# A ninth weight buffer in the place of the transposed activations, and cache pages looked up four at a time

## The chip, the cores and the metric

The kernel runs on one core of a Trainium2 chip. The metric is device time in microseconds (us) of one execution, and each kernel is timed in several runs whose median counts. Five engines work side by side, each through its own queue of instructions in order: TensorE (PE, with its weight loads PEld), VectorE (DVE), ScalarE (ACT), GpSimd (POOL) and SyncE (SP). SP here only issues DMA transfers and looks up the addresses that they need. SBUF is the on-chip memory in which tiles lie, PSUM the memory into which TensorE writes.

## The reference

One step of a hybrid decoder layer on 288 tokens: 256 of a prompt and 8 requests of 4 new tokens each. Cut to what matters here:

```python
u = rmsnorm(h, g_mix)
q_lat, q_rope, lat, k_rope, x_br, y_br = mixer_projections(u, ...)
# prompt: causal attention over its 256 tokens
# samples: 16 cached pages of 128 positions per request, found by a page table
lat_past = cache_latent[page_table]; rope_past = cache_krope[page_table]
s = (q_lat @ lat.T + q_rope @ k_rope.T) * SM_SCALE
o_lat = softmax(s) @ lat
o_rec = rglru(causal_conv(x_br))               # a recurrence over the tokens
h = h + concat(rmsnorm(o_mla), rmsnorm(gelu(y_br) * o_rec)) @ w_o
# 32 experts of three 2048 x 512 matrices; each token uses 2 of them
h = h + sum_e combine[:, e] * (silu(t @ w_gate[e]) * (t @ w_up[e])) @ w_down[e]
h = h + sigmoid(rmsnorm(h) @ w_ple_gate + b) * (p @ w_ple_proj)
y = rmsnorm(h)
```

The outputs are y, the new latent rows and rotated keys, and the last states of the recurrence and of the convolution. All is float32; the expert matrices alone are 403 MB, read once.

## The kernel before

**Front part (0 to 470 us).** The dense projections run as products of 128 x 128 weight blocks with 288 token columns. A weight tile of 512 KB is loaded into `wraw` (`load`, L207; three buffers), split into a high and a low part (`whi` by ACT, L219; `wlo` by DVE, L220), and three matmuls per block (L229 to L231) add up the product: 24 matmuls for each `wraw` tile. After each tile `dense3` calls `hook`, and with it `tick`, which lets other work in: steps of the recurrence, and the sample attention.

The sample attention has 16 units (`sample`, `fetch`), one started every second tick. A unit takes four requests and two pages of each: 8 pages of 288 KB, read into four `kv` buffers out of 12 (`KVB`). For each page SP reads its number out of the page table (L488) and issues the DMA (L490). Then TensorE computes scores `Ss` (L503, L507), DVE and ACT make the softmax (`ms`, `Ssb`; L512 to L532), TensorE transposes it (`tp`, L538), DVE copies it out (`pTs`, L539) and TensorE multiplies it with the page (`Os`, L550). These names are the ones in the rows below; `pg`, `xc`, `gr`, `gi`, `yb` and `xx` belong to the recurrence.

In this part a scheduler orders the instructions of every engine while the program is built, from the order of the calls and its own idea of what is ready; the queues then run in that order.

At its end the residual `hT` (128 x 16 x 288, 18 KB per partition) holds h, token columns side by side. `post` (L902, L908) reads each of its 16 blocks once more: for the router's logits, and to transpose it into `hn`, in which tokens are rows. After that nothing reads or writes `hT` until the down projections add to it.

**Expert part (470 to 1100 us).** Experts are taken in ten units, 0 to 9: units 0, 3, 5 and 7 hold two experts (wide), the others four. `front` runs over four quarters of the 2048 inputs, first for `w_gate`, then for `w_up`; `wload` takes the next slot of a ring (`slots`, `wslot`) and issues a DMA of 2 MB for two experts (L1012). The ring has eight slots: five in a pool that opens when the front part's operands are released (`ws1`, w0 to w4), two more in a pool behind them (`ws3`), and one where the router's small tiles lay (`ws4`). A slot is loaded again when TensorE has read it. `gather` picks each expert's tokens out of `hn` with one-hot matmuls (`xp`, L1054). Small jobs are put in between by two lists: `front` takes one entry of `steps` per block under `w_gate`, one of `more` under `w_up`. Behind unit `OVU` (3) stands `overflow`, a branch that is taken only if an expert has more tokens than its place holds; it reads a flag on every engine (L1225).

**Down part (1100 to 1452 us).** `down` reads `w_down` through the ring's five `ws1` slots and adds to `hT` (L1131); here TensorE's order is as written. The last 47 us are the gated embedding and the final norm.

Of the kernel before, what the change touches and what calls it, by code (L numbers as in the profile page):

```python
# [21 lines left out]
NP = 256  # L22
# [12 lines left out]
KVB = 12  # L35
AHEAD = 2
NSQ = 2
NNQ = 0
# [8 lines left out]
HEAVY = 4  # L47
OVU = 3
XXW = 3 + NP + 7 * NR
# [67 lines left out]
def hymba_kernel(ctx, tc, a):  # L117
# [53 lines left out]
    tmp = pool(st_tmp, "tmp")  # L171
    wps = [pool(st_w, "wp"), 3, 3, 2]
    up = pool(st_u, "up")
# [4 lines left out]

    lane, queue, clock = [], [], [0]

    def tick():

        for g in list(lane):
            if next(g, 1):
                lane.remove(g)
        if queue:
            clock[0] += 1
            if clock[0] <= AHEAD or (clock[0] - AHEAD) % PACE == 0 or clock[0] >= DENSE:
                start()
# [125 lines left out]
    dma(C, a["cst"])  # L315
    ptk = za.tile([1, 128], I32, name="ptk")
    dma(ptk, a["table"])
    uh = up.tile([128, KD, NTOK], F32R, name="uh")
# [140 lines left out]

    sa = pool(st_sa, "sa")  # L460
    pq = psF([128, 2, H, 32], "pq")

# [16 lines left out]
    last = [None] * 2  # L479

    def fetch(u):
        g, v = divmod(u, 8)
        L = []
        for j in range(4):
            kv = sa.tile([128, 2, 576], F32, name="kv", bufs=KVB)
            for x in range(2):
                c = 16 * (4 * g + j) + 2 * v + x
                page = nc.values_load(ptk[0:1, c:c + 1], engines=[mybir.EngineType.SP], min_val=0,  # L488
                                      max_val=a["cache"].shape[0] - 1)
                dma(kv[:, x, :], a["cache"][bass.ds(page, 1)].rearrange("o p c -> (o p) c"))  # L490
            L.append(kv)
        return L

    def sample(u):

        L = fetch(u)
        g, v = divmod(u, 8)
# [65 lines left out]
    def finish(g, m):  # L563
# [20 lines left out]
    def prompt_pool():  # L584
# [9 lines left out]
        for b in range(2):  # L594
            wuvp.append([pa.tile([128, 2, 4, 128], F32R, name="wv" + nm) for nm in "hl"])
            halves(*wuvp[b], wuv[:, :, 4 * b:4 * b + 4, :])
            for t in range(2):
                p = psK([128, 512], "vv")
                for c in range(2):
                    x = [y[:, c, t * 128:(t + 1) * 128] for y in lp_]  # L600
                    mm3(p, *x, *(y[:, c].rearrange("p h v -> p (h v)") for y in wuvp[b]), c == 0, c == 1)
                nc.scalar.copy(vv[:, t, 4 * b:4 * b + 4, :].rearrange("p h v -> p (h v)"), p)
            r = pa.tile([128, 2, 4, 128], F32, name="wr")
            dma(r, a["wuk"][:, :, 4 * b:4 * b + 4, :])
            wk.append([pa.tile([128, 2, 4, 128], F32R, name="wk" + nm, bufs=2) for nm in "hl"])
            halves(*wk[b], r)
            yield
# [101 lines left out]
    class Part:  # L709
# [19 lines left out]
        def begin(self):  # L729
            n = self.n  # L730
            self.xs = self.xx[:, :, 3 + NP:].rearrange("p c (r s) -> p c r s", s=7)
            self.cvs = lp.tile([128, 2, NR, 3], F32, name="cvs")
            self.xc = lp.tile([128, 2, CW], F32, name="xc")
# [6 lines left out]
                "p c (r s) -> p c r s", s=3))  # L740
            nc.vector.tensor_copy(self.cvs, self.xs[:, :, :, 4:])

        def conv(self, c):
# [19 lines left out]
        def decay(self):  # L763
            n = self.n
            dma(cp_d[:, 2 * n:2 * n + 2], self.xx[:, :, NP:3 + NP])
            dma(cs_d[:, 2 * n:2 * n + 2], self.cvs)
            gr, t2, th = self.gr, self.t2, self.th
            nc.scalar.activation(th, gr, AF.Tanh)
            nc.scalar.activation(t2, gr, AF.Exp, scale=2.0)
            nc.scalar.activation(gr, gr, AF.Exp)  # L770
            nc.vector.scalar_tensor_tensor(t2, t2, 1.0, th, op0=ALU.add, op1=ALU.mult)
# [13 lines left out]
        def state(self):  # L785
# [4 lines left out]
            if n == 3:  # L790
                dma(a["lru_p"], lrp[:, :8])
                dma(a["lru_s"], lrp[:, 8:])

        def gelu(self):
# [130 lines left out]
    ws3 = pool(st_w3, "ws3")  # L925
    slots = [(ws1, f"w{i}") for i in range(WB1)] + [(ws3, f"w{WB1 + i}") for i in range(WB3)]

# [72 lines left out]
    def wslot(i=0):  # L1000
        p_, nm = slots.pop(i)
        return p_.tile([128, 2, 4, 512], F32, name=nm), (p_, nm)

# [215 lines left out]

    more += [lambda: None] * 4 + [lambda: reorder(rkT, rks), limits, weights]  # L1220

# [386 lines left out]
def layout(inp):  # L1608
# [16 lines left out]
    for n in range(4):  # L1625
# [13 lines left out]
        cr.reshape(-1, 2, 64, 64).transpose(0, 1, 3, 2).reshape(-1, 128, 64), cl], 2)  # L1639
    A["table"] = f["page_table"].reshape(1, -1)  # L1640
    w = f["w_o"][0]
# [48 lines left out]
```

## Time and profile before

| | us |
|---|---|
| median of 3 runs (1497.66 to 1500.59) | 1499.51 |
| the profiled execution's own time | 1500.35 |
| its span, first to last instruction | 1498.7 |
| TensorE busy | 1300.5 (87%) |
| VectorE, ScalarE busy | 553.5, 392.0 |
| mean traffic | 346 GB/s over the span |

The span is 1.65 us shorter than the time, and the profiled execution is 0.84 us above the median. Engines work at once, so busy times don't add up to the span. "Idle before" is time in which an engine did nothing right before an instruction, with what it waited for last. A DMA's share of 1.00 means that all 16 DMA engines were busy throughout.

### The profile page before, as it was taken

To read this page: it belongs to the slowest core of one execution; us is meant where nothing else is said; L and a number is where in the kernel's file an instruction comes from. 1 tells how busy PE (TensorE), PEld (TensorE's weight loads), DVE (VectorE), ACT (ScalarE), POOL (GpSimd) and SP (SyncE) were. 2 spreads that over 40 slices of the span, in tenths; PEclk is the share of its full clock that TensorE was granted. 3 is DMA by queue.
4 is the path that set the end of the run, shared out by engine and by line. 5 is a ranking of instruction groups with operands and counts; after the bars stand their busy time and mean duration, and the time that the engine had idled before them with its cause. 6 is when DMAs were issued, how large, how long until landed. Compare 5 with 4: busy or idle time off the path is not lost.

```text
span 1498.7 us, 24037 instructions
## 1 busy us (share of the span) xinstructions
PE 1300.5 (87%) x9535; PEld 851.1 (57%) x9535; DVE 553.5 (37%) x1322; ACT 392.0 (26%) x744; POOL 23.1 (2%) x26
## 2 busy tenths in 40 slices
PE   7999888799999988775978868869778999999996
PEld 7997677588996444222523423416235666666675
DVE  6765545666663100000000000003023455555557
ACT  6535434655441100000000000002013322222335
POOL 0000000000000000000000000000000000000014
PEclk9999998999999999987999989979899999999997
DMA  7879787532776899999999999999999999999971
GB/s 271 275 242 295 240 277 246 160 141 76 266 273 266 352 396 427 428 427 428 417 428 427 428 428 427 427 426 426 393 418 419 419 419 419 419 419 418 420 287 64
DMA packets 80841, 518.32 MB, mean 346 GB/s; under 512 B 10705, under 2 KB 12818, under 8 KB 47826
## 3 DMA queue, kind: packets, MB, share of 16 engines
q1 hardware_dynamic: 80066, 514.33, 86.3%
q0 software_dynamic: 656, 2.39, 0.4%
q8 instruction: 77, 1.26, 0.3%
q14 instruction: 42, 0.34, 0.1%
HBM read 513.81 MB, written 2.88 MB: 345 GB/s over the span
## 4 chain that ended last, share of the span: by engine, by line
DMA 35%; PE 15%; DVE 2%; issue 1%; ACT 0%; DVEq 0%; SPq 0%; ACTq 0%
DMA w<-in_w_down 21%; DMA w<-in_w_up 8%; PE Gp L1081 6%; DMA w<-in_w_gate 5%; PE xp L1054 4%; PE Y L1114 2%; PE pp L1280 1%; DMA wpp<-in_w_pp 1%; DVE gtt L1492 1%; DVE hT L1495 0%; DVE gtt L1487 0%; DVE hT L1596 0%; PE yp L1129 0%; PE s L1464 0%; PE acc L1460 0%
## 5 line engine op out<-in xcount | busy, mean ns | idle before, releaser
L1081 PE MATMUL Gp<-w,Xq 128*32 128x512 f32 (+1 forms) x2048 | 356.8, 673 | 93.4 <-DMA w<-in_w_up 50.1
L1081 PEld LDWEIGHTS Gp<-w,Xq 128*32 128x32 f32 (+1 forms) x2048 | 89.7, 127 | 318.7 <-issue 175.9
L229 PE MATMUL acc<-uh,whi 128*128 128x288 f32 x496 | 155.6, 314 | 14.9 <-ACT whi L219 7.4
L231 PE MATMUL acc<-uh,wlo 128*128 128x288 f32 x496 | 153.8, 310 | 3.5 <-DVE wlo L220 3.4
L230 PE MATMUL acc<-ul,whi 128*128 128x288 f32 x496 | 152.4, 307 | 0.4 <-DVE ul L264 0.4
L1090 DVE SCALAR_TENSOR_TENSOR Yb<-Gp,rs,Yb 128x512 f32<-128x512 f32 x10 | 7.5, 751 | 341.8 <-PE Gp L1081 307.5
L1131 DVE TENSOR_TENSOR hT<-hT,yp 128x288 f32<-128x288 f32 x160 | 71.2, 450 | 165.2 <-PE yp L1129 165.2
L1054 PE MATMUL xp<-Pq,hn 96*128 96x256 f32 (+1 forms) x576 | 119.8, 360 | 12.8 <-issue 12.0
L1114 PE MATMUL Y<-w,w 128*32 128x256 f32 (+1 forms) x1280 | 113.8, 389 | 19.2 <-DMA w<-in_w_down 19.1
L1054 PEld LDWEIGHTS xp<-Pq,hn 96*128 96x128 f32 x576 | 97.2, 197 | 53.9 <-issue 42.6
L229 PEld LDWEIGHTS acc<-uh,whi 128*128 128x128 f32 x496 | 97.9, 197 | 19.0 <-ACT whi L219 9.2
L220 DVE TENSOR_TENSOR wlo<-wraw,whi 128x1024 fp32r<-128x1024 f32 x82 | 99.9, 1220 | 18.6 <-PE acc L231 9.8
L231 PEld LDWEIGHTS acc<-uh,wlo 128*128 128x128 f32 x496 | 98.0, 198 | 7.4 <-DVE wlo L220 5.8
L219 ACT CAST whi<-wraw 128x1024 fp32r<-128x1024 f32 x82 | 85.4, 1042 | 63.9 <-PE acc L230 45.5
L230 PEld LDWEIGHTS acc<-ul,whi 128*128 128x128 f32 x496 | 98.2, 198 | 1.6 <-DVE ul L264 0.9
L1114 PEld LDWEIGHTS Y<-w,w 128*32 128x32 f32 (+1 forms) x1280 | 51.7, 116 | 66.2 <-DMA w<-in_w_down 34.1
L1058 DVE TENSOR_SCALAR Xq<-xp,P 128x256 f32<-128x256 f32 (+1 forms) x48 | 21.1, 440 | 168.5 <-PE xp L1054 168.5
L1118 ACT ACTIVATE Yh<-Y,wsl 128x256 fp32r<-128x256 f32 x80 | 37.9, 473 | 173.6 <-PE Y L1114 172.9
L1089 ACT ACTIVATE Yb<-Gp,rs 128x512 f32<-128x512 f32 x10 | 6.9, 687 | 283.9 <-PE Gp L1081 278.4
L1114 PE MATMUL Y<-w,wl 128*32 128x256 f32 (+1 forms) x768 | 72.3, 389 | 8.9 <-DMA w<-in_w_down 8.9
L1056 ACT ACTIVATE Xq<-xp,P 128x256 f32<-128x256 f32 (+1 forms) x48 | 21.0, 438 | 189.8 <-PE xp L1054 189.8
L231 PE MATMUL acc<-gh,wlo 128*128 128x288 f32 x224 | 66.1, 295 | 1.3 <-DVE wlo L226 1.3
(487 smaller groups left out, 1868.8 us busy)
## 6 DMA issues: line engine op xcount, KB each, us to landing
w<-in_w_gate SPq DMA_DIRECT2D x64, 2048.0 KB, 26.0
w<-in_w_up SPq DMA_DIRECT2D x64, 2048.0 KB, 24.8
w<-in_w_down SPq DMA_DIRECT2D x128, 1024.0 KB, 17.1
kv<-in_cache SPq DMA_DIRECT2D x128, 288.0 KB, 3.9
wraw<-in_w_in SPq DMA_DIRECT2D x44, 512.0 KB, 4.8
wraw<-in_w_o SPq DMA_DIRECT2D x32, 512.0 KB, 4.0
wraw<-in_w_pg SPq DMA_DIRECT2D x30, 512.0 KB, 15.2
wraw<-in_w_uq SPq DMA_DIRECT2D x6, 512.0 KB, 4.1
```

What stands on the lines that cost most here:

```text
L219: nc.scalar.copy(hi[:, x, :], r[:, x, :])
L220: nc.vector.tensor_sub(lo[:, x, :], r[:, x, :], hi[:, x, :].bitcast(F32))
L229: nc.tensor.matmul(out, hi, xh, start=start, stop=False)
L230: nc.tensor.matmul(out, hi, xl, start=False, stop=False)
L231: nc.tensor.matmul(out, lo, xh, start=False, stop=stop)
L1054: nc.tensor.matmul(xp, hn[:, t, d * 128:(d + 1) * 128], Pq[:, t, :n], start=t == 0, stop=t == 2)
L1056: nc.scalar.activation(X[:, d, :n], xp, AF.Copy, scale=prm("g_ffn", d))
L1058: nc.vector.tensor_scalar(X[:, d, :n], xp, prm("g_ffn", d), None, op0=ALU.mult)
L1081: nc.tensor.matmul(acts[j][sl * e:sl * e + sl, :], X[:, kk, o:o + sl], wt[e](k), start=kk == 0, stop=kk == KD - 1)
L1114: nc.tensor.matmul(Y[sl * e:sl * e + sl, :], at[:, f, sl * e:sl * e + sl], w(f), start=f == 0, stop=f == 3)
L1118: nc.scalar.activation(Yh, Y, AF.Copy, scale=ws)
L1131: nc.vector.tensor_add(h_, h_, yp)
```

## The change

Three parts, in one edit.

1. **A ninth slot.** The first 16 KB per partition of `hT` become a slot of the ring, between `ws1`'s five and `ws3`'s two. At unit 7 (`OVU` is now 7) the slot leaves the ring, and `restore` transposes `hn` back into `hT` block by block: 48 transposes and 16 copies, put into `more`. The overflow branch, which adds to `hT`, moves from behind unit 3 to behind unit 7. The jobs `limits` and `weights` stand 13 entries later in `more`, in unit 1 instead of unit 0.
2. **Pages in fours.** The page table is laid out unit by unit and clamped once by DVE; one SP instruction reads four page numbers into four registers, without a check of each. A unit's pages are asked for one unit ahead, in two halves that `tick` issues one per call.
3. **Smaller moves.** `wraw` has four buffers instead of three and also takes the two `wuk` tiles (before: a buffer of their own, `wr`). The convolution's last states are collected in two tiles and written by two DMAs at the end of the recurrence, instead of eight within it.

```diff
-OVU = 3
+OVU = 7
...
-    wps = [pool(st_w, "wp"), 3, 3, 2]
+    wps = [pool(st_w, "wp"), 4, 3, 2]
...
         for g in list(lane):
             if next(g, 1):
                 lane.remove(g)
+        for _ in range(min(PAGES // 4, len(loads))):
+            loads.pop(0)()
...
+    nc.vector.tensor_scalar(ptk, ptk, 0, a["cache"].shape[0] - 1, op0=ALU.max, op1=ALU.min)
...
+        fetched[u] = [sa.tile([128, 2, 576], F32, name="kv", bufs=KVB) for _ in range(4)]
+
+        def page(j0):
+            o = 8 * u + 2 * j0
+            _, ns = nc.values_load_multi_w_load_instructions(
+                ptk[0:1, o:o + 4], engines=[mybir.EngineType.SP], min_val=0, max_val=a["cache"].shape[0] - 1,
+                skip_runtime_bounds_check_because="clamped above")
+            for i, n in enumerate(ns):
+                dma(fetched[u][j0 + i // 2][:, i % 2, :], a["cache"][bass.ds(n, 1)].rearrange("o p c -> (o p) c"))
+        loads.extend(lambda j=j: page(j) for j in (0, 2))
...
-        L = fetch(u)
+        fetch(u)
+        flush()
+        L = fetched[u]
+        fetch(u + 1)
...
-            r = pa.tile([128, 2, 4, 128], F32, name="wr")
+            r = wps[0].tile([128, 8, 128], F32, name="wraw", bufs=wps[1]).rearrange("p (c h) v -> p c h v", c=2)
...
-            dma(cp_d[:, 2 * n:2 * n + 2], self.xx[:, :, NP:3 + NP])
-            dma(cs_d[:, 2 * n:2 * n + 2], self.cvs)
...
-    slots = [(ws1, f"w{i}") for i in range(WB1)] + [(ws3, f"w{WB1 + i}") for i in range(WB3)]
+
+    slots = [(ws1, f"w{i}") for i in range(WB1)] + [(None, "hT")] + [(ws3, f"w{WB1 + i}") for i in range(WB3)]
...
+        if p_ is None:
+            return hT.rearrange("p k t -> p (k t)")[:, :4096].rearrange("p (e k f) -> p e k f", e=2, k=4), (p_, nm)
...
-    more += [lambda: None] * 4 + [lambda: reorder(rkT, rks), limits, weights]
+    more += [lambda: None] * 4 + [lambda: reorder(rkT, rks)] + [lambda: None] * 13 + [limits, weights]
+
+    def restore(c):
+
+        p = psB([128, 3, TT], "hb")
+        for t in range(3):
+            nc.tensor.transpose(p[:, t, :], hn[:, t, c * 128:(c + 1) * 128], con("ident", rows=TT, hi=TT))
+        if c % 2:
+            nc.scalar.copy(hT[:, c, :], p.rearrange("p t q -> p (t q)"))
+        else:
+            nc.vector.tensor_copy(hT[:, c, :], p.rearrange("p t q -> p (t q)"))
...
+            if u == OVU:
+                slots[:] = [x for x in slots if x[0] is not None]
+                more += [lambda c=c: restore(c) for c in range(KD)]
```

The change also shifts the order that the scheduler finds. On TensorE, at the scores and the softmax transposes (`tp`) of the sixth sample unit, stood before:

```order
L550 MATMUL Os<-kv,pTs 32x256 x8
L503 MATMUL Ss<-kv,qls 32x256 x8
L507 MATMUL Ss<-kv,qrs 32x2x64 x8
L229 MATMUL acc<-uh,whi 128x288
L230 MATMUL acc<-ul,whi 128x288
L538 MATMUL tp<-C,Ssb 128x128 x2
L231 MATMUL acc<-uh,wlo 128x288
L229 MATMUL acc<-uh,whi 128x288
L230 MATMUL acc<-ul,whi 128x288
```

The same transposes now (24 `acc` rows stand between the scores' last row and them; the last three are shown):

```order
L232 MATMUL acc<-uh,whi 128x288
L233 MATMUL acc<-ul,whi 128x288
L234 MATMUL acc<-uh,wlo 128x288
L554 MATMUL tp<-C,Ssb 128x128 x2
L519 MATMUL Ss<-kv,qls 32x256 x2
L232 MATMUL acc<-uh,whi 128x288
L233 MATMUL acc<-ul,whi 128x288
L566 MATMUL Os<-kv,pTs 32x256 x7
```

Between scores and transposes two `acc` rows have become 24; between the transposes and `Os` 46 have become two, with two score rows of the next unit.

On SP, a page in the sample attention took these rows before (two pages shown):

```order
L488 TENSOR_LOAD ptk
L488 ISA x2
L490 ISA
L490 DMA kv<-in_cache 128x576
L488 TENSOR_LOAD ptk
L488 ISA x2
L490 ISA
L490 DMA kv<-in_cache 128x576
```

Now four pages take these:

```order
L496 TENSOR_LOAD ptk
L500 ISA
L500 DMA kv<-in_cache 128x576
L500 ISA
L500 DMA kv<-in_cache 128x576
L500 ISA
L500 DMA kv<-in_cache 128x576
L500 ISA
L500 DMA kv<-in_cache 128x576
```

One lookup stands for four, and two register rows per page are gone; in the later units a `wraw` load follows each such group.

On SP at the start of the expert part, where the first eight tiles and the ninth are issued (with the slots' numbers), stood before:

```order
L1012 DMA w4_6472<-in_w_gate 128x4096
L1012 DMA w5_6502<-in_w_up 128x4096
L1012 DMA w6_6512<-in_w_gate 128x4096
L1012 DMA w7_6532<-in_w_up 128x4096
L1173 TENSOR_LOAD ids_6346
L1173 ISA x2
L1012 ISA
L1012 DMA w0_6575<-in_w_gate 128x4096
```

And now:

```order
L1037 DMA w4_5458<-in_w_gate 128x4096
L1037 DMA w5_5497<-in_w_gate 128x4096
L1037 DMA hT_3522<-in_w_up 128x4096
L1037 DMA w6_5517<-in_w_up 128x4096
L1198 TENSOR_LOAD ids_5351
L1198 ISA x2
L1037 ISA
L1037 DMA w7_5560<-in_w_gate 128x4096
L1198 TENSOR_LOAD ids_5351
L1198 ISA x2
L1037 ISA
L1037 DMA w0_5572<-in_w_gate 128x4096
```

One more tile stands ahead of the first reused slot, w0. On TensorE the `restore` transposes (`hb`) come out at the beginning of unit 7:

```order
L1118 MATMUL ap__6899<-C,Yb 128x128 x4
L1251 MATMUL hb<-C,hn 128x96 x2
L1106 MATMUL Gp<-w_6917,Xq 64x512 x8
L1251 MATMUL hb<-C,hn 128x96 x30
L1106 MATMUL Gp<-w_6927,Xq 64x512 x8
L1251 MATMUL hb<-C,hn 128x96 x16
L1110 MATMUL rsp<-r_4473,Pq 128x1 x3
```

All 48 stand within the first two of the unit's eight tiles.

## Rows read from the trace of the kernel before

**Rows 1.** Busy time by stage: stretch in us from the span's start, its length, then busy us (and instructions) of each engine, TensorE's granted clock as a share of full speed, the DMA engines' busy share and GB/s.

```profile
115.00:305.00 190.00, 162.11 (x1373) 130.90 (x1365) 108.41 (x264) 92.26 (x149) 0.00 (x0) 0.92 0.76 241
305.00:470.00 165.00, 162.87 (x1211) 152.00 (x1210) 103.45 (x247) 75.27 (x151) 0.00 (x0) 1.00 0.52 190
540.00:1040.00 500.00, 399.63 (x2230) 173.93 (x2226) 40.18 (x136) 34.78 (x72) 2.81 (x5) 0.91 1.01 427
1040.00:1100.00 60.00, 44.60 (x292) 15.49 (x284) 1.39 (x3) 3.73 (x8) 0.00 (x0) 0.89 0.96 402
1100.00:1452.00 352.00, 322.70 (x2987) 216.87 (x2984) 179.81 (x415) 91.58 (x185) 0.56 (x1) 0.99 1.01 416
```

**Rows 2.** The head of the chain of waits that ended last: shares of the span by line.

```profile
by line: DMA w<-in_w_down 21.5%; DMA w<-in_w_up 8.3%; PE Gp L1081 6.2%; DMA w<-in_w_gate 4.5%; PE xp L1054 3.9%; PE Y L1114 1.9%; PE pp L1280 1.0%; issue 0.8%; DMA wpp<-in_w_pp 0.8%; DVE gtt L1492 0.6%; DVE hT L1495 0.5%; DVE gtt L1487 0.4%
```

**Rows 3.** SP's issues of expert tiles at the start of the expert part, in order of time: start in us, duration, line, transfer.

```profile
437.99 0.43 SPq L1012 DMA_DIRECT2D w<-in_w_gate  x1
455.94 0.33 SPq L1012 DMA_DIRECT2D w<-in_w_up  x1
456.31 0.44 SPq L1012 DMA_DIRECT2D w<-in_w_gate  x1
470.61 0.33 SPq L1012 DMA_DIRECT2D w<-in_w_up  x1
476.87 0.34 SPq L1012 DMA_DIRECT2D w<-in_w_gate  x1
```

**Rows 4.** Busy time in stretches of 20 us at the same place; columns as in rows 1.

```profile
440.00:460.00 20.00, 19.90 (x174) 19.71 (x174) 10.42 (x23) 7.67 (x15) 0.00 (x0) 1.00 0.42 161
460.00:480.00 20.00, 19.03 (x128) 12.16 (x126) 9.30 (x53) 1.89 (x6) 0.00 (x0) 1.00 0.78 297
480.00:500.00 20.00, 20.00 (x105) 9.25 (x103) 2.59 (x10) 1.49 (x4) 0.00 (x0) 1.00 0.93 365
500.00:520.00 20.00, 18.24 (x94) 9.45 (x92) 2.21 (x7) 3.29 (x5) 0.00 (x0) 0.93 0.91 370
520.00:540.00 20.00, 20.00 (x167) 9.70 (x170) 1.75 (x5) 1.84 (x5) 0.00 (x0) 0.98 0.84 342
```

**Rows 5.** What TensorE waited for from 115 to 305 us: us in total, times, longest.

```profile
PE tp L538 <- ACT Ssb L526: 11.5, 7, 1.9
PE acc L229 <- ACT whi L219: 8.8, 6, 2.2
PE acc L231 <- DVE wlo L220: 3.4, 5, 0.9
PE tp L570 <- DVE Obs L567: 1.7, 2, 1.1
PE ssy L280 <- DVE accy L273: 1.1, 1, 1.1
PE Os L550 <- DVE pTs L539: 0.5, 1, 0.5
PE pg L756 <- ACT gr L757: 0.5, 3, 0.2
```

**Rows 6.** TensorE in order of time at two places of that stretch; in brackets the idle time before, and what ended it.

```profile
225.79 0.44 PE L538 MATMUL tp<-C,Ssb 128*128 128x128 f32 x2 [1.68 <-ACT Ssb L526]
226.75 0.68 PE L550 MATMUL Os<-kv,pTs 128*32 128x256 f32 x2 [0.52 <-DVE pTs L539]
...
293.12 0.44 PE L570 MATMUL tp<-C,Obs 128*128 128x128 f32 x2 [1.08 <-DVE Obs L567]
294.94 0.40 PE L229 MATMUL acc<-ul,whi 128*128 128x288 f32 x1 [1.38 <-ACT whi L219]
296.58 1.12 PE L280 MATMUL ssy<-ones,accy 128*96 128x1 f32 x6 [1.11 <-DVE accy L273]
299.08 0.61 PE L231 MATMUL acc<-ul,wlo 128*128 128x288 f32 x1 [0.69 <-DVE wlo L220]
```

**Rows 7.** The rows of SP's page lookups and page transfers: engine, operation, count, duration in ns (least, median, most), first and last start; then the transfers' time to landing in us.

```profile
L488 SPq TENSOR_LOAD <-ptk x128: 262/268/482, 23.5 to 262.6; - x128
L488 SPq FUSED_REGOPS  x128: 147/152/181, 24.0 to 262.9; - x128
...
L490 SPq FUSED_REGOPS  x128: 37/37/48, 36.3 to 263.2; - x128
L490 SPq MOVE kv<-in_cache x128: 29/29/42, 36.3 to 263.3; - x128
L490 SPq DMA_DIRECT2D kv<-in_cache x128: 332/333/1150, 36.4 to 263.3; - x128
...
DMA to landing us min/median/max: 2.7/3.9/6.2
```

**Rows 8.** SP in order of time: the eight pages of one unit.

```profile
131.59 8.24 SPq L490 DMA_DIRECT2D kv<-in_cache  x8
```

**Rows 9.** First the transposes of `post`: count, duration in ns (least, median, most), first and last start. Then groups of instructions by form: the same transposes, their copies, and ACT's table loads ahead of the softmax exponential; busy us, mean ns of one, then idle before.

```profile
L908 PE MATMUL tph<-C,hT x48: 272/273/293, 401.0 to 458.2; 128*96 128x128 f32 x48
...
L908 PE MATMUL tph<-C,hT 128*96 128x128 f32 x48 | 8.3, 279 | 0.0
L909 ACT COPY hn<-tph 96x384 f32<-96x384 f32 x16 | 7.6, 474 | 21.0 <-PE tph L908 21.0
L526 ACT ACT_TABLE_LOAD x4 | 5.1, 1283 | 3.2 <-DVE ms L525 3.2
```

**Rows 10.** TensorE and SP around the overflow branch behind unit 3, in order of time; and unit 7's stretch (columns as in rows 1).

```profile
690.26 0.33 SPq L1012 DMA_DIRECT2D w<-in_w_up  x1
...
703.78 1.44 PE L1054 MATMUL xp<-Pq,hn 96*128 96x256 f32 x3 [11.98 <-issue]
...
718.69 1.16 SPq L1012 DMA_DIRECT2D w<-in_w_gate  x2
...
880.00:900.00 20.00, 15.23 (x76) 5.06 (x76) 2.12 (x8) 1.11 (x2) 0.00 (x0) 0.83 1.00 425
900.00:920.00 20.00, 15.44 (x70) 4.52 (x68) 0.00 (x0) 0.00 (x0) 0.00 (x0) 1.00 1.01 430
```

More of the change, by code (lines that the diff above doesn't have):

```diff
@@ L36 @@
 AHEAD = 2
+PAGES = 4
 NSQ = 2
@@ L177, in hymba_kernel @@
     hooks = []
-    lane, queue, clock = [], [], [0]
+    lane, queue, clock, loads = [], [], [0], []
     def tick():
@@ L315, in hymba_kernel @@
     dma(C, a["cst"])
-    ptk = za.tile([1, 128], I32, name="ptk")
-    dma(ptk, a["table"])
     uh = up.tile([128, KD, NTOK], F32R, name="uh")
@@ L460, in hymba_kernel @@
     sa = pool(st_sa, "sa")
+    ptk = sa.tile([1, 128], I32, name="ptk")
+    dma(ptk, a["table"])
+    nc.vector.tensor_scalar(ptk, ptk, 0, a["cache"].shape[0] - 1, op0=ALU.max, op1=ALU.min)
     pq = psF([128, 2, H, 32], "pq")
@@ L479, in hymba_kernel, with flush @@
     last = [None] * 2
+    fetched = {}
     def fetch(u):
+        if u in fetched or u > 15:
+            return
         g, v = divmod(u, 8)
[L483 to L492, printed above, removed]
+        fetched[u] = [sa.tile([128, 2, 576], F32, name="kv", bufs=KVB) for _ in range(4)]
[7 more added lines that the diff above has]
+        loads.extend(lambda j=j: page(j) for j in (0, 2))
+    def flush():
+        while loads:
+            loads.pop(0)()
     def sample(u):
-        L = fetch(u)
+        fetch(u)
+        flush()
+        L = fetched[u]
+        fetch(u + 1)
         g, v = divmod(u, 8)
@@ L573, in finish @@
                                   tp[:, c * 128:(c + 1) * 128].rearrange("p (j h t) -> p h j t", j=4, h=H))
+    fetch(0)
+    flush()
+    fetch(1)
     for u in range(16):
@@ L684, in hymba_kernel @@
     hb = lp.tile([128, 16], F32, name="hb")
+    cvp = lp.tile([128, 8, 3], F32, name="cvp")
+    cvs = lp.tile([128, 8, NR, 3], F32, name="cvs")
     c4 = sp[4]
@@ L731, in begin @@
             self.xs = self.xx[:, :, 3 + NP:].rearrange("p c (r s) -> p c r s", s=7)
-            self.cvs = lp.tile([128, 2, NR, 3], F32, name="cvs")
+            self.cvs = cvs[:, 2 * n:2 * n + 2]
             self.xc = lp.tile([128, 2, CW], F32, name="xc")
@@ L741, in begin @@
             nc.vector.tensor_copy(self.cvs, self.xs[:, :, :, 4:])
+            nc.vector.tensor_copy(cvp[:, 2 * n:2 * n + 2], self.xx[:, :, NP:3 + NP])
         def conv(self, c):
@@ L792, in state @@
                 dma(a["lru_s"], lrp[:, 8:])
+                dma(cp_d, cvp)
+                dma(cs_d, cvs)
         def gelu(self):
@@ L1639, in layout @@
         cr.reshape(-1, 2, 64, 64).transpose(0, 1, 3, 2).reshape(-1, 128, 64), cl], 2)
-    A["table"] = f["page_table"].reshape(1, -1)
+    A["table"] = np.ascontiguousarray(f["page_table"].reshape(2, 4, 8, 2).transpose(0, 2, 1, 3)).reshape(1, -1)
     w = f["w_o"][0]
```

## The prediction

> **What bounds the kernel now.** First the busy time by stage [rows 1]: the reader is to see two regimes. From 115 to 470 us TensorE is what is busy (162.1 of 190 us and 162.9 of 165 us) while the DMA engines run at a share of 0.76 and 0.52. From 540 to 1452 us it is the other way round: the DMA share is 1.01 at 427 and 416 GB/s, and TensorE has gaps. Then the chain of waits that ended last [rows 2], which in this second regime is made of transfers of expert weights (21.5% + 8.3% + 4.5% of the span). So a microsecond saved on TensorE after 540 us is worth nothing, and what counts is when the stream of weights starts and whether it ever pauses. Before 470 us it is TensorE's own gaps that count, since the pools for the first weights open only when its work is done. Last, the 20 us stretches at the seam [rows 4]: between 460 and 540 us the DMA share is 0.78, 0.93, 0.91 and 0.84, so the stream is not yet saturated there; 4.4 + 1.4 + 1.8 + 3.2 = 10.8 us of DMA time go unused.
>
> **The ninth slot.** A slot holds 2 MB (2,097,152 bytes); at the 427 GB/s of the saturated stretch that is 4.9 us of the stream. Before, SP issues two tiles at 455.9 and 456.3 us, the next only at 470.6 and the first reused slot at 476.9 [rows 3]. Two tiles keep the stream busy to about 466 us, so a third, into `hT`, whose last transposes start at 458.2 us [rows 9], falls into an idle stretch of some 4.5 us. The later slots come free when TensorE has read them, at the same times as before, so from there on the stream is one tile ahead, and where it saturates, at about 540 us, it has 4.9 us less to do. The share of 1.01 from there to 1040 and of 1.01 from 1100 to 1452 [rows 1] says that nothing gives this back; the dip from 1040 to 1100 (0.96) is a wait for small tiles of the embedding, which I leave as it is. Term: **-4.9 us**. Bounds: 0 if the tile collides with another, -10.8 if all of the seam's unused time goes (a little of it can, since `limits` and `weights` leave unit 0).
>
> The Trainium skill, page "DMA: Bandwidth & Descriptors", section "Specifications", states an HBM limit of about 358 GB/s for a core. By it the tile would be worth 5.9 us and the sum 1 us lower. The trace disagrees with the page: 427 GB/s [rows 1], and the measurement decides.
>
> **What the ninth slot costs.** `restore` adds 48 transposes, as many as `post` has, which keep TensorE busy for 8.3 us; its 16 copies of about 0.47 us are shared by ACT and DVE [rows 9], which have nothing else to do there (1.1 and 2.1 us busy in 20). They stand in unit 7, where TensorE is idle for 4.8 and 4.6 us in 20 us [rows 10]. What hides them is the ring: eight slots in flight are 39 us of stream. The branch, now behind the same unit, has a price on TensorE: 12.0 us without a matmul, and SP issues no tile from 690.3 to 718.7 us, 28.4 us [rows 10]; yet the DMA share of the stage stays 1.01, since 28.4 is under 39. With 8.3 us more it would be 36.7, still under 39. Term 0; if that cover is short, up to +8.3.
>
> **Pages in fours.** Before, a page costs SP a lookup of 0.268 us, register work of 0.152, 0.037 and 0.029 and an issue of 0.333 us [rows 7]; eight take 8.24 us [rows 8], a little over the 6.6 us that these add up to. After, eight pages keep 8 x 0.40 = 3.2 us and two lookups: at least 0.5 us, 2.1 if a lookup costs 0.268 per register. So SP gets back 3 to 4.5 us a unit, some 60 us in all. By itself this is worth nothing: in what TensorE waits for there is no page at all, and only converted weights, `whi` and `wlo` [rows 5], not transfers. What it changes is the order that the scheduler finds.
>
> **The new order in the front.** From 115 to 305 us TensorE is idle for 190 - 162.1 = 27.9 us, and its granted clock averages 0.92, that is, part of the time it is at the lower of its levels (1.2 instead of 2.4 GHz): 0.08 x 190 = 15.2 us more [rows 1]. The largest wait is the softmax transposes' for the exponential: 11.5 us in 7 places, 1.64 each [rows 5]. In the order of before nine units have at most two `acc` matmuls between scores and transposes: these seven, and two in which the `acc` matmul in between waited instead. In the new order I count four (units 6, 8, 10 and 12 of 0 to 15); the others have 14 to 24 in between. Seven to four: 3 x 1.64 = **-4.9 us**. The passage to the prompt's attention has waits of 1.08, 1.38, 1.11 and 0.69 us [rows 6]; in the new order more `acc` rows stand between these steps, and I take half: **-2.1 us**. Against this, `Os` now stands within four matmuls of its transposes in nine places instead of one; that one waited 0.52 us [rows 6]: 8 x 0.52 = **+4.2 us**. ACT loads a table right before the exponential seven times instead of four, at 1.28 us [rows 9]; in the three new places 24 matmuls stand in between, so I count nothing (bound: +3.8). The clock's share goes with the waits: 2.8 of 27.9 is 10%, of 15.2 that is **-1.5 us**. Together **-4.3 us**. Nothing of this is behind other work: the next 165 us are solid TensorE work [rows 1], so what is gained arrives at the seam. Bounds: -43 if all waits and the whole clock loss went, which no reordering does, and about +13 if the eight new `Os` places cost 2.2 us each, the longest wait in rows 5, and nothing else went (8 x 2.2 - 4.9). The value lies near the counted places, since these have a price from rows.
>
> The small moves (four DVE copies more, six small issues fewer, a fourth `wraw` buffer where no transfer is waited for) I put at 0.
>
> **Sum.** 1500.35 - 4.9 - 4.3 = 1491.2 for an execution like the profiled one. The median stands 0.84 lower, so I forecast 1490.3, rounded **1490 us**.
>
> **Rivals.**
> *The front gains far more.* If SP's long page blocks were behind the late conversions too, half of idle time and clock loss would go: (27.9 + 15.2) / 2 = 21.5, and 1500.35 - 4.9 - 21.5 = 1474. For it: `whi` and `wlo` are 12.2 of the 27.5 us in rows 5, and a `wraw` load behind eight pages can be 8 us late. Against: these waits name ACT and DVE, not a transfer. 0.2.
> *Nothing arrives.* The order swaps its waits one for one, and the ninth slot's lead is lost when the slot leaves the ring before the branch: 1498 to 1501. For it: both orders come from the same scheduler, and the one of before holds 43 us of waits and slow clock. Against: a lead in a saturated stream is bytes already there. 0.15.
> *Slower: the second half of the pages comes late.* The new order splits the scores, two matmuls ahead and six after 22 `acc` matmuls, as it would if the second four pages arrived only then. They are issued one tick after the first. SP's 1.9 us and a landing of 3.9 us [rows 7] stand against 22 matmuls of cover, 3.0 us at 162.87 / 1211 = 0.134 us each [rows 1]; each of 11 split units would wait 2.8 us: +31, so 1500.35 - 4.9 + 31 = 1526. It decides once the wait is over 0.8 us per unit (9.2 / 11). Against: SP runs ahead of TensorE by up to four `wraw` tiles, and before, with 8.24 us per unit, no page was waited for. 0.13.
> The Trainium skill, page "Runtime: NRT & Kernel Launch", section "Instruction fetch mechanics", says that loading registers costs about 200 ns each, in bulk too. A lookup of four would then be an estimated 0.8 us and SP's half unit 2.4 us; that rule speaks for this last rival and makes its wait 0.5 us longer. No lookup of four is in this trace; the single one agrees (0.268 us, rows 7).
>
> **How the numbers follow.** Forecast 0.5, rivals 0.2, 0.15 and 0.13, the rest (a drained ring at the branch) 0.02. The forecast's own range is 1482 to 1497. The range for 8 in 10 takes in most of the first rival and the second: 1475 to 1502; below it lies some of the first rival, above it the third. A measurement can tell 0.2%, 3 us, from no change. Faster by more: nearly all of the forecast (0.47), the first rival (0.2), a little of the second (0.05) make 0.72. Within 0.2%: 0.03 of the forecast, 0.09 of the second, 0.02 of the third with a short wait, 0.14. Slower: 0.14.
>
> **What would show it.** The ninth slot: at the seam three tiles issued near 456 to 459 us, counted from the front's end, the unused DMA time about 5 us smaller, and a distance from the front's last `post` transpose to the end of the down part that is 5 us shorter. The front: that transpose (458 us before) about 5 us earlier, fewer transposes that wait for `Ssb`, more `Os` that wait for `pTs`. The branch: a DMA share of 1.0 through units 7 and 8. I am wrong if `Ss` waits for pages, if the DMA share drops behind unit 7, or if the front ends no earlier.

## The result, and the profile after

The changed kernel takes 1489.28 us (median of 4 runs, 1488.55 to 1492.00) against 1499.90 of the kernel before (4 runs, 1497.66 to 1500.59): a ratio of 0.9936, with a 95% interval of 0.9923 to 0.9950. The forecast was 1490. The sum is right; what it is made of is not, as the experiments show. The profiled execution has a span of 1487.1 us against 1498.7. Two executions, one of the kernel before at 3046.94 us and one of the kernel with pages not asked for ahead at 1521.50 us, lie far above all others of their kernels and are left out of the medians and ratios below (with the second, that kernel's median would be 1485.93, the figure that later expectations name).

First the head of the chain of waits that ended last, from the page of the changed kernel.

```profile
DMA w<-in_w_down 21%; PE Gp L1106 3%; PE Y L1139 2%; DMA w<-in_w_up 2%; PE xp L1079 2%; DMA w<-in_w_gate 1%; PE pp L1315 1%; DMA wpp<-in_w_pp 1%; DVE gtt L1530 1%; DVE hT L1533 0%; PE s L1502 0%; DVE gtt L1525 0%; DVE hT L1634 0%; PE yp L1154 0%; PE acc L1498 0%
```

It is still made of weight transfers, as [rows 2]. Next, busy time by stage, with the stretches and columns of [rows 1].

```profile
115.00:305.00 190.00, 169.05 (x1412) 132.31 (x1405) 108.94 (x272) 94.13 (x153) 0.00 (x0) 0.97 0.71 247
305.00:470.00 165.00, 163.20 (x1202) 150.49 (x1202) 101.63 (x245) 72.76 (x147) 0.00 (x0) 0.99 0.54 202
540.00:1040.00 500.00, 406.86 (x2275) 179.35 (x2273) 43.56 (x143) 38.83 (x82) 2.81 (x5) 0.92 1.00 424
1040.00:1100.00 60.00, 46.99 (x346) 17.07 (x345) 5.03 (x12) 3.74 (x8) 0.00 (x0) 0.83 1.00 414
1100.00:1452.00 352.00, 325.00 (x2977) 222.96 (x2977) 185.41 (x428) 97.65 (x197) 6.21 (x5) 0.99 0.97 402
```

From 115 to 305 us TensorE's idle time fell from 27.9 to 20.9 us, and the mean granted clock rose from 0.92 to 0.97. From 540 us the DMA engines are busy throughout; the 0.97 in the last row is only the stream's earlier end. Then SP's tile issues at the seam, in order of time, as [rows 3].

```profile
448.50 0.33 SPq L1037 DMA_DIRECT2D w<-in_w_gate  x1
449.20 0.33 SPq L1037 DMA_DIRECT2D hT<-in_w_up  x1
449.58 0.42 SPq L1037 DMA_DIRECT2D w<-in_w_up  x1
463.99 5.93 SPq L1037 DMA_DIRECT2D w<-in_w_gate  x2
```

Three tiles now leave within 1.1 us, the middle one into `hT`, where there were two. What TensorE waited for from 115 to 305 us, with the columns of [rows 5]:

```profile
PE acc L234 <- DVE ms L541: 5.2, 4, 1.8
PE tp L554 <- ACT Ssb L542: 4.7, 2, 2.8
PE acc L232 <- ACT whi L222: 4.3, 4, 1.3
PE acc L234 <- DVE wlo L223: 3.1, 3, 1.3
PE pg L778 <- ACT gr L779: 2.1, 6, 0.3
PE Os L566 <- DVE pTs L555: 1.0, 2, 0.5
```

The transposes' wait went from 11.5 us in 7 places to 4.7 in 2, that for `whi` from 8.8 to 4.3. The first row is new. The page lookup and the page issue, as [rows 7]:

```profile
L496 SPq TENSOR_LOAD <-ptk x32: 296/302/515, 35.7 to 244.4; - x32
...
L500 SPq DMA_DIRECT2D kv<-in_cache x128: 332/333/1344, 36.4 to 248.7; - x128
```

A lookup of four takes 0.302 us, hardly more than one of one (0.268). Last, unit 7: the `restore` transposes (`hb`) as one group; then the busy time of all instructions that write or read `hb`, in the order TensorE, its weight loads, VectorE, ScalarE; then, each in order of time, TensorE and SP around the branch, as [rows 10].

```profile
L1251 PE MATMUL hb<-C,hn x48: 243/246/302, 878.4 to 889.8; 96*128 96x96 f32 x48
```

```profile
870.00:900.00 30.00, 4.65 (x48) 4.21 (x48) 3.66 (x8) 3.18 (x8) 0.94 1.01 427
```

```profile
923.25 4.61 PE L1079 MATMUL xp<-Pq,hn 96*128 96x256 f32 x10 [7.23 <-DVE Pq L1063]
...
914.48 23.44 SPq L1037 DMA_DIRECT2D w<-in_w_up  x2
```

The 48 transposes keep TensorE busy for 4.65 us, and not 8.3: one lasts 0.246 us, but they overlap. In the last row, between its first and second issue, SP is silent for some 23 us.

Where did the 11.6 us between the two spans come from? The last `post` transpose starts at 450.8 us instead of 458.2: 7.4 us. From there to the start of the last down matmul it is 987.8 us instead of 992.9: 5.1. The tail is 0.9 longer. By this the front gave more than forecast and the ring about as much. That reading is wrong, as the experiments show.

### The profile page after: what moved, and what is told of

It reads as the page before. It is cut to its first block, busy times and chain, and to the rows that moved or that the text cites. A ratio compares the mean times of both kernels' runs of the same rounds, so it can differ in the third digit from the quotient of the medians.

```text
span 1487.1 us, 23803 instructions
## 1 busy us (share of the span) xinstructions
PE 1307.4 (88%) x9583; PEld 853.3 (57%) x9583; DVE 555.2 (37%) x1335; ACT 395.4 (27%) x752; POOL 23.1 (2%) x26
## 5 line engine op out<-in xcount | busy, mean ns | idle before, releaser
L1106 PE MATMUL Gp<-w,Xq 128*32 128x512 f32 (+1 forms) x1888 | 340.9, 675 | 77.5 <-DMA w<-in_w_gate 39.8
L1106 PEld LDWEIGHTS Gp<-w,Xq 128*32 128x32 f32 (+1 forms) x1888 | 84.5, 127 | 280.4 <-issue 161.2
L232 PE MATMUL acc<-uh,whi 128*128 128x288 f32 x496 | 154.3, 311 | 11.6 <-ACT whi L228 6.5
## 6 DMA issues: line engine op xcount, KB each, us to landing
wraw<-in_w_pg SPq DMA_DIRECT2D x30, 512.0 KB, 15.2
```

The source lines that it names most:

```text
L232: nc.tensor.matmul(out, hi, xh, start=start, stop=False)
L1106: nc.tensor.matmul(acts[j][sl * e:sl * e + sl, :], X[:, kk, o:o + sl], wt[e](k), start=kk == 0, stop=kk == KD - 1)
```

## The experiments

**Each part alone, and the first part undone.** First the changed kernel without its first part; up to the last `post` transpose its order is the changed kernel's on every engine.

```diff
-OVU = 7
+OVU = 3
...
-    slots = [(ws1, f"w{i}") for i in range(WB1)] + [(None, "hT")] + [(ws3, f"w{WB1 + i}") for i in range(WB3)]
+    slots = [(ws1, f"w{i}") for i in range(WB1)] + [(ws3, f"w{WB1 + i}") for i in range(WB3)]
...
-    more += [lambda: None] * 4 + [lambda: reorder(rkT, rks)] + [lambda: None] * 13 + [limits, weights]
+    more += [lambda: None] * 4 + [lambda: reorder(rkT, rks), limits, weights]
...
-                more += [lambda c=c: restore(c) for c in range(KD)]
```

> The changed kernel without its first part: eight slots, no restore, the branch behind unit 3, limits and weights in unit 0. TensorE's order up to the last post transpose is that of the changed kernel. By my theory the ninth slot is worth 4.9 us of stream and costs nothing; in the two traces the distance from that transpose to the end of the span is 1040.5 us before and 1036.3 us after, 4.2 us less. So 1489.3 + 4.2 to 4.9 = 1493.5 to 1494.2. If the slot gives nothing and all is the front's, 1489.3; if the slot gives all, 1499.9.

Measured: 1497.28 us (12 runs, 1493.69 to 1501.20), 0.9982 of before, interval 0.9970 to 0.9993. The kernel before took 1499.82 us beside it (22 runs). So the first part gives 8.0 us (1497.28 - 1489.28) and the other two 2.5 together; by the interval these two give 1.0 to 4.5. In this run's profile the last `post` transpose is at 457.3 us, not 450.8.

The second kernel is the opposite: before, with that edit's lines the other way round.

> The kernel before with the first part alone. TensorE's order up to the last post transpose is that of before. By my theory 1499.9 - 4.2 to 4.9 = 1495.0 to 1495.7, with that transpose still at 458 us and the distance from it to the end at 1036. If the slot's lead is lost at the branch, 1499.9.

Measured: 1491.42 us (6 runs, 1490.87 to 1492.61), 0.9943, interval 0.9929 to 0.9957: 8.4 us, more than either expectation. From the last `post` transpose (457.5) to the end it is 1032.5 us.

The third is before with the pages in fours alone:

```diff
+    nc.vector.tensor_scalar(ptk, ptk, 0, a["cache"].shape[0] - 1, op0=ALU.max, op1=ALU.min)
...
-        L = fetch(u)
+        fetch(u)
+        flush()
+        L = fetched[u]
+        fetch(u + 1)
```

> The kernel before with the second part alone (pages in fours, asked for a unit ahead). By my theory the pages change the order and so the front's waits: the last post transpose comes 7.4 us earlier, as in the changed kernel, and the time is 1499.9 - 7.4 = 1492.5. If the front's gain came from the fourth wraw buffer and the other small moves, 1499.9. If each order is a new draw, anything between 1490 and 1505, and the waits of TensorE from 115 to 305 us say how much.

Measured: 1508.00 us (6 runs, 1506.43 to 1508.44), 1.0052, interval 1.0037 to 1.0066: slower by 8, outside all three. The last `post` transpose is at 463.8 us.

The fourth is before with the small moves alone:

```diff
-    wps = [pool(st_w, "wp"), 3, 3, 2]
+    wps = [pool(st_w, "wp"), 4, 3, 2]
...
-            r = pa.tile([128, 2, 4, 128], F32, name="wr")
+            r = wps[0].tile([128, 8, 128], F32, name="wraw", bufs=wps[1]).rearrange("p (c h) v -> p c h v", c=2)
...
-            dma(cs_d[:, 2 * n:2 * n + 2], self.cvs)
...
+                dma(cs_d, cvs)
```

> The kernel before with the third part alone (four wraw buffers, wuk through them, the convolution's states in two DMAs). By my theory no change, 1499.9. If the fourth buffer is what took the waits for whi away (8.8 us before, 4.3 us after), 1499.9 - 4.5 = 1495.4 or less, down to 1492.5.

Measured: 1501.18 us (12 runs, 1498.22 to 1507.34), 1.0016, interval 1.0002 to 1.0030. The waits for `whi` did fall, from 8.8 to 2.7 us, but the transposes' rose from 11.5 to 15.5. The parts of the front don't add up: +8.2 and +1.4 apart, -2.5 together (each against 1499.82).

**What else the first part moved.** Its two other edits, each alone on the kernel before:

```diff
-OVU = 3
+OVU = 7
```

> The kernel before with the branch behind unit 7 instead of 3, no ninth slot. The first part as a whole gave 8.6 us on the kernel before, where the unused DMA time at the seam that it takes away is 4.4 us. Theory A, the slot alone gives all of it: no change, 1500.0. Theory B, the rest of some 4 us comes from the branch's new place: 1496.

Measured: 1499.53 us, 1.0000 of before, interval 0.9990 to 1.0009. The branch's place is worth nothing.

```diff
-    more += [lambda: None] * 4 + [lambda: reorder(rkT, rks), limits, weights]
+    more += [lambda: None] * 4 + [lambda: reorder(rkT, rks)] + [lambda: None] * 13 + [limits, weights]
```

> The kernel before with limits and weights 13 entries later (in unit 1), eight slots. Theory A, the slot alone counts: no change, 1500.0. Theory C, the rest of some 4 us comes from unit 0, where TensorE is the bound, being relieved of this work: 1496 to 1498.

Measured: 1499.91 us, 1.0006, interval 0.9997 to 1.0015: nothing either. So the slot itself gives the 8 us. A slot less tells how:

```diff
-WB3 = 2
+WB3 = 1
```

> The kernel before with seven slots instead of eight (one buffer of the pool behind the operands left out). If a slot is worth its 2 MB of stream, 4.4 to 4.9 us: 1500.0 + 4.4 to 4.9 = 1504.4 to 1504.9, with that much more unused DMA time within 80 us of the front's end. If a slot is worth more than its bytes, as the 8.6 us of the first part suggest: 1508 or above, with DMA pauses later than that.

Measured: 1514.52 us (4 runs, 1512.08 to 1515.98), 1.0102, interval 1.0087 to 1.0118: 15.5 us slower. Where these go is read from stretches of 100, 400, 60 and 100 us counted from each kernel's last `post` transpose; columns as in [rows 1]. The kernel before:

```profile
458.20:558.20 100.00, 94.31 (x622) 48.98 (x621) 18.85 (x89) 11.09 (x25) 0.00 (x0) 0.98 0.89 360
558.20:958.20 400.00, 321.95 (x1720) 138.51 (x1720) 25.15 (x63) 23.58 (x45) 0.00 (x0) 0.91 1.01 427
...
1018.20:1118.20 100.00, 80.31 (x564) 38.11 (x567) 14.33 (x55) 13.27 (x31) 1.05 (x2) 0.93 0.98 411
```

With seven slots:

```profile
459.90:559.90 100.00, 93.32 (x611) 49.18 (x614) 18.84 (x89) 11.12 (x25) 0.00 (x0) 0.97 0.84 339
559.90:959.90 400.00, 314.58 (x1685) 132.88 (x1678) 24.34 (x61) 22.69 (x43) 0.00 (x0) 0.92 1.00 422
...
1019.90:1119.90 100.00, 78.08 (x509) 37.72 (x510) 14.04 (x66) 13.31 (x32) 1.06 (x2) 0.88 0.95 393
```

Before with the ninth slot:

```profile
457.50:557.50 100.00, 95.83 (x634) 49.90 (x637) 18.82 (x89) 11.10 (x25) 0.00 (x0) 0.97 0.94 382
557.50:957.50 400.00, 321.56 (x1736) 138.40 (x1730) 28.09 (x69) 26.33 (x52) 0.00 (x0) 0.92 1.01 427
957.50:1017.50 60.00, 45.61 (x300) 19.91 (x293) 7.88 (x34) 5.26 (x12) 1.76 (x3) 0.91 1.00 419
1017.50:1117.50 100.00, 79.89 (x593) 36.79 (x596) 15.73 (x56) 12.42 (x29) 1.05 (x2) 0.93 1.00 420
```

The last column is read first. In the first 100 us the rates are 339, 360 and 382 GB/s: each step is 21 or 22, that is 2.1 or 2.2 MB, one tile. But the slot's cover pays later as well. With seven the 400 us that hold the branch lose 5 GB/s (400 x 5 / 427 = 4.7 us), and the last stretch, in which the pools change for the embedding, falls from 411 to 393 (100 x 18 / 419 = 4.3 us): 4.9 + 4.7 + 4.3 = 13.9 us, as the distance from the last `post` transpose to the last down matmul says (1006.7 - 992.9 = 13.8). The ninth slot gains that tile and, in the last stretch, 9 GB/s (2.1 us); behind the branch, in the 60 us, the stream pauses a little, at 419 GB/s.

**The cover behind the branch.** `restore` done twice in the changed kernel:

```diff
     def restore(c):
+        for r_ in range(2):
+            again(c)
+
+    def again(c):
```

> The changed kernel with every step of restore done twice in unit 7 (96 transposes and 32 copies instead of 48 and 16). Theory A, the ring hides them: no change, 1489.3, with the DMA share through units 7 and 8 as it was. Theory B, the nine-slot ring has no cover left beside the branch, as the dip to 0.91 in 5 us behind it suggests: the added TensorE time of some 4.7 us (48 of 0.1 us) shows in full, 1494.

Measured: 1491.44 us (6 runs, 1486.17 to 1496.11) beside 1490.09 (6 runs, 1487.70 to 1496.95) for the changed kernel on the same chip: 1.3 us apart. The added steps keep TensorE busy for 5.4 us more (10.03 for `hb` instead of 4.65). The spread of the runs is too wide to exclude that these show in full; the distance from the last `post` transpose to the last down matmul speaks against it: 987.3 us, within the 983.9 to 987.8 of six kernels with nine slots and `restore` done once, and 1.7 above their mean. The 60 and 100 us stretches of it, counted as above:

```profile
954.20:1014.20 60.00, 46.94 (x310) 19.83 (x309) 7.90 (x34) 5.12 (x12) 1.76 (x3) 0.91 0.97 406
1014.20:1114.20 100.00, 81.00 (x592) 37.43 (x590) 15.66 (x56) 13.04 (x30) 1.06 (x2) 0.95 1.01 423
```

Theory A's reason falls as well: the stream does pause behind the branch (406 GB/s, against 418 to 425 in the other six). But the next stretch runs at 423, where those have 410 to 420: the pause at the embedding is gone. The kernel with eight slots and the branch behind unit 7, which has no `restore` at all, shows the same pause in the same 60 us:

```profile
958.70:1018.70 60.00, 46.38 (x310) 19.96 (x309) 7.38 (x31) 4.36 (x9) 1.76 (x3) 0.91 0.99 413
```

The kernel before has 426 GB/s there. In the next 100 us the two run at 413 and 411, and their times are the same. In these profiles a lead lost at one stall did not have to be lost again at the next.

**The front, again.** The changed kernel once more, unchanged:

> The changed kernel once more, for its time beside the three above and for a second profile. In its first profile the last post transpose ended at 451 us, 7.4 us before that of the kernel before; in the one without the ninth slot, whose front has the same order on all engines, at 457.3 us. Theory A, the order saves some 2 us and the rest was one execution with fewer stretches at the lower clock: median 1489.3, the transpose anywhere from 451 to 458. Theory B, the 7.4 us are the order's: the transpose at 451 again.

Measured: 1490.09 us, 0.9941 of before, interval 0.9919 to 0.9962, and the last `post` transpose at 455.4 us. With 450.8 and 457.3, and 454.2 with `restore` doubled, that makes four executions of one order of TensorE up to there. Their idle time from 115 to 305 us agrees (20.9 or 21.0 us); their clock does not: 0.97 with 450.8, 0.96 with 454.2, 0.95 with 455.4, 0.94 with 457.3. Five profiles have the order of the kernel before (itself, the ninth slot alone, the branch late, `limits` late, seven slots): 454.9 to 459.9 us, at a clock of 0.94 to 0.92. The means are 454.4 and 457.8 us, so 3.4 of the first profile's 7.4 us are the order's by these nine, and the rest is that execution's. The kernel without the first part, from 115 to 305 us:

```profile
115.00:305.00 190.00, 169.07 (x1391) 131.89 (x1379) 105.28 (x262) 91.11 (x149) 0.00 (x0) 0.94 0.68 235
```

TensorE is idle for 20.9 us there as in the changed kernel's first profile, but the clock is 0.94 and not 0.97, and 0.03 x 190 = 5.7 us of the 6.5 between the two are explained by this. One place shows it: the longest of its waits, in order of time, and busy time in 4 us beside it, first in the changed kernel's first profile, then in this one.

```profile
237.98 0.44 PE L554 MATMUL tp<-C,Ssb 128*128 128x128 f32 x2 [2.82 <-ACT Ssb L542]
```

```profile
239.00:243.00 4.00, 4.00 (x31) 2.83 (x32) 2.73 (x3) 2.27 (x4) 0.00 (x0) 1.00 0.44 157
```

```profile
240.07 0.69 PE L554 MATMUL tp<-C,Ssb 128*128 128x128 f32 x2 [2.82 <-ACT Ssb L542]
```

```profile
241.00:245.00 4.00, 3.72 (x17) 1.36 (x17) 2.90 (x4) 2.37 (x4) 0.00 (x0) 0.50 0.49 162
```

The same wait of 2.82 us is followed by 31 matmuls at 2.4 GHz in one execution and by 17 at 1.2 GHz in the other. What the order itself changes is seen in the scores and `Os`. Groups up to the last `post` transpose: busy us, mean ns of one, idle before. The kernel before:

```profile
L503 PE MATMUL Ss<-kv,qls 128*32 128x256 f32 x256 | 21.7, 382 | 0.0
L550 PE MATMUL Os<-kv,pTs 128*32 128x256 f32 x256 | 18.7, 399 | 0.5 <-DVE pTs L539 0.5
L507 PE MATMUL Ss<-kv,qrs 128*32 128x128 f32 x256 | 11.9, 273 | 0.0
```

The changed kernel:

```profile
L519 PE MATMUL Ss<-kv,qls 128*32 128x256 f32 x256 | 26.5, 387 | 0.0
L566 PE MATMUL Os<-kv,pTs 128*32 128x256 f32 x256 | 22.1, 397 | 1.0 <-DVE pTs L555 1.0
L523 PE MATMUL Ss<-kv,qrs 128*32 128x128 f32 x256 | 16.0, 274 | 0.0
```

As many matmuls, about as long each, but longer busy times. The three can't be added up, for matmuls of `qls` and `qrs` run at the same time (below, at 205.76 and 205.78). So the busy time of all instructions that write or read `Ss`, then `Os`, up to the last `post` transpose (TensorE first, then its weight loads, VectorE, ScalarE). The kernel before:

```profile
0.00:458.20 458.20, 28.70 (x512) 17.09 (x512) 6.72 (x16) 9.00 (x32) 0.97 0.68 227
0.00:458.20 458.20, 19.91 (x260) 7.57 (x260) 7.55 (x16) 0.97 0.68 227
```

The changed kernel:

```profile
0.00:450.80 450.80, 33.43 (x512) 18.30 (x512) 6.77 (x16) 9.03 (x32) 0.98 0.66 230
0.00:450.80 450.80, 23.38 (x260) 8.21 (x260) 7.57 (x16) 0.98 0.66 230
```

That is 56.8 us of TensorE instead of 48.6: 8.2 us more. A unit's `Ss` matmuls write four different strips of 32 rows and overlap, as 16 of 0.38 us in 1.05 us show. Where the order takes a unit apart, overlap is lost. One unit of the changed kernel in order of time, its first piece at 200.12:

```profile
200.12 0.63 PE L519 MATMUL Ss<-kv,qls 128*32 128x256 f32 x4
...
205.09 0.84 PE L519 MATMUL Ss<-kv,qls 128*32 128x256 f32 x10
205.56 0.39 PE L523 MATMUL Ss<-kv,qrs 128*32 128x128 f32 x4
205.76 0.39 PE L519 MATMUL Ss<-kv,qls 128*32 128x256 f32 x2
205.78 0.81 PE L523 MATMUL Ss<-kv,qrs 128*32 128x128 f32 x12
```

A whole unit of the kernel before:

```profile
207.79 1.05 PE L503 MATMUL Ss<-kv,qls 128*32 128x256 f32 x16
208.65 0.62 PE L507 MATMUL Ss<-kv,qrs 128*32 128x128 f32 x16
```

In two pieces the unit takes 0.63 + 1.50 = 2.13 us, in one 1.48. Twelve of 16 units are split after, five before.

The Trainium skill, page "TensorE: Matmul & The Clock Gate", section "Part 3: Packing small matmuls — row/col tiling", says that small matmuls on different 32 x 32 tiles of the array run at the same time. The trace agrees, by the 16 in 1.05 us.

The kernel with the pages alone bears the price out. Twelve of its units are split too, its `Ss` and `Os` take 34.63 + 24.04 = 58.7 us, 10.1 more than before, and TensorE's idle time up to the last `post` transpose is that of the kernel before (37.7 and 37.8 us): nothing is saved against the price, and it is 8 us slower.

If that is the price, a front that asks for no page ahead should be better. The edit leaves the lookup in fours, and issues a unit's eight pages when it starts:

```diff
-        for _ in range(min(PAGES // 4, len(loads))):
-            loads.pop(0)()
```

> The changed kernel with pages still looked up four at a time, but all eight of a unit issued when the unit starts, none a tick ahead. In its order 6 of the 16 units' scores are split in pieces with acc matmuls between them, against 12 of 16 in the changed kernel; a split unit's scores take 0.62 + 1.50 us there, against 1.50 in one piece. My theory now: the changed kernel loses some 12 us to longer scores and Os (33.6 + 18.7 us of TensorE before, 42.5 + 22.1 after) and this gives half of it back, 1489.3 - 6 = 1483 or a little more, since two softmax transposes more stand close behind their scores (1.6 us each): 1483 to 1486. If asking ahead is what gained, the front is that of before and the time 1491.4, as with the ninth slot alone.

Measured: 1484.2 us (median of 4 runs, 1482.50 to 1486.16), 0.9910 of before, interval 0.9894 to 0.9925: faster than both kernels, as expected. The last `post` transpose is at 448.5 us, and `Ss` and `Os` take 47.3 us, 1.3 less than before; the views are those above:

```profile
0.00:448.50 448.50, 27.66 (x512) 17.05 (x512) 6.73 (x16) 9.03 (x32) 0.97 0.66 232
0.00:448.50 448.50, 19.60 (x260) 7.48 (x260) 7.54 (x16) 0.97 0.66 232
```

The order differs in other places too (idle time from 115 to 305 us is 23.1 us, and not 20.9), so what the splits alone are worth is not isolated by this run.

Two more kernels place the lookup and the fourth buffer. The changed kernel without its second part:

```diff
-        fetch(u)
-        flush()
-        L = fetched[u]
-        fetch(u + 1)
+        L = fetch(u)
```

> The changed kernel without its second part: each page looked up by itself in its own unit, ninth slot and small moves kept. The front's order on TensorE is that of the kernel with the small moves alone (1501.2 us). If the parts add up, 1501.2 - 8 to 8.6 = 1492.6 to 1493.2. Beside the changed kernel (1489.3) and the one with fours not ahead (1485.9) this tells what the lookup in fours is worth: some 7 us against single lookups in the same place, and half of that given back by asking ahead. If the lookup is worth nothing by itself, as my prediction had it, 1486 to 1489.

Measured: 1494.18 us (9 runs, 1490.32 to 1496.15), 0.9968, interval 0.9958 to 0.9979. The forecast of additive parts was a little low. Beside the small moves the pages are worth 4.1 us (1494.18 - 1490.09), without them they cost 8.

The kernel with fours not ahead, with three `wraw` buffers:

```diff
-    wps = [pool(st_w, "wp"), 4, 3, 2]
+    wps = [pool(st_w, "wp"), 3, 3, 2]
```

> The kernel with fours not ahead (1485.9) with three wraw buffers instead of four; the scores are split in the same places. Theory A, no load of wraw is waited for: no change, 1484 to 1488. Theory B, the fourth buffer is part of the gain: waits for whi and wlo rise from 8.9 us by 3 or more, 1489 or above.

Measured: 1488.15 us (6 runs, 1484.38 to 1491.63). The waits for `whi` and `wlo` rose from 8.9 to 11.4 us. TensorE's idle time from 115 to 305 us rose from 23.1 to 24.9 us, where executions of one and the same order agree within 0.6. The ranges overlap, the two ran on different chips and their orders are not quite the same, so this is not settled, but it leans to theory B.

## Why the prediction was right, and where it was not

**The time** was right in part by luck, because two errors cancelled: the ninth slot gave some 8 us instead of 4.9, the front some 2 to 3 instead of 4.3 (2.5 without the slot; with it 1491.42 against 1489.28 or 1490.09, which is 1.3 to 2.1). The first error is clear; the second is not clear of the noise (1.0 to 4.5).

**The ninth slot, -4.9.** The seam came as forecast: three tiles at once, and 21 GB/s more over 100 us, one tile. The step that failed is the sentence that leaves the dip from 1040 to 1100 us "as it is". From the last `post` transpose to the last down matmul the six profiles with eight slots show 991.6 to 993.5 us (mean 992.8), the six unmodified in unit 7 with nine 983.9 to 987.8 (mean 985.6): 7.2 us. About 1.7 of the excess is the dip: 405 to 413 GB/s over those 100 us in the eight-slot profiles (mean 409), 410 to 420 in the nine-slot ones (mean 416). Some 0.5 goes back behind the branch (418 to 425 GB/s in the 60 us ahead of the dip, where eight slots with the branch behind unit 3 had 425 or 426). In the kernel before TensorE spends 19.3 us on the embedding's `pp` from 1010 to 1058 us, and from 1018 us on SP waits up to 14.6 us for `Gp` to have read a slot: such a stall is what a slot more covers. The last microsecond I have no row for.

**Its cost, 0.** The branch at 0 was right (ratio 1.0000), and so was `limits` and `weights` at 0 or little (1.0006). `restore` is not felt, but it is little more than half as long as put (4.65 us), and the reason given, 39 us of ring against a silence of 28.4 or 36.7, was not what decides: behind unit 7 SP is silent for some 23 us only, and the stream pauses all the same, at 413 GB/s with eight slots and no `restore`, at 418 to 425 with nine, at 406 with `restore` doubled. What is lost there is not seen in the time; in the next 100 us these profiles run faster than their likes (413 GB/s against a mean of 409 with eight slots, 423 against 416 with nine).

**Pages in fours.** SP's part was right: by the sum 8 x 0.40 + 2 x 0.302 = 3.8 us a unit, in the forecast bounds of 3.7 and 5.3. In order of time four issues in a row take 1.95 us (at 114.69 us), with the lookup 2.25, so a unit some 4.5 us, still within them. The Trainium skill, page "Runtime: NRT & Kernel Launch", section "Instruction fetch mechanics", puts a register at about 200 ns in bulk too. The trace disagrees: four in 0.302 us.

**The new order in the front, -4.3.** The `tp` term was -4.9 for seven places to four; it became -6.8, for two are left. The passage, -2.1: its waits for `Obs` (1.7 us) and `accy` (1.1) are gone. `Os`, +4.2: only +0.5, since most of the nine places do not wait. Not foreseen: 5.2 us of `acc` for which the trace names DVE's `ms`, and 4.5 less for `whi`. Together idle time fell by 7.0 us. The step that failed is the method: it priced the order by waits alone, and split scores show no wait. `Ss` and `Os` take 8.2 us more, which is more than the idle time gives back; by these rows what is left of the front's gain is the clock's. The clock, -1.5, was sized too small: at 0.92 to 0.94 it costs 15.2 to 11.4 us in the order of before, at 0.94 to 0.97 it costs 11.4 to 5.7 in the new one (0.08 x 190 = 15.2, and so on). This varies from execution to execution by more than the front's whole gain.

**The rivals.** A front that gains far more did not come; the 7.4 us of the first profile are 3.4 in the mean of nine. Nothing arrives: the front's gain is indeed small, but the ninth slot's lead was not lost when the slot left the ring, as its 8 us show. The slower rival saw the right place, scores taken apart with `acc` between, and the wrong mechanism: it is overlap that is lost, and no page is late (no wait for a page stands among TensorE's in the changed kernel's front). Alone, the pages did make the kernel slower, by 8 us.

## What to carry to other kernels

A buffer more in a saturated stream is worth its bytes once, and again at each later stall that it covers; count the stalls, not only the start. When an edit lets a scheduler find another order, look at busy time as well as at waits, and over all groups that can run at the same time, or some of it is counted twice: small matmuls that overlap lose it silently when they are taken apart. Compare two fronts over several executions, or with the front held fixed, before a difference in one profile is called the edit's.

## What was not expected of the hardware

After one and the same wait of 2.82 us, in one and the same order, the granted clock stayed at 1.00 in one execution and fell to 0.50 in another; the front's end moved between 450.8 and 457.3 us with it. A lookup of four page numbers took 0.302 us, one of one 0.268. And 48 transposes of 0.246 us each kept TensorE busy for 4.65 us only.
